# Summing the modulation vectors over the partitions by accumulating DMAs instead of by products with ones, in the first FFN of a two-layer diffusion backbone

## The chip, the cores and the metric

The kernel runs on one core of a Trainium2 chip. The metric is the device time of one execution in microseconds (us). The kernel before takes 1251.65 us, the median of three runs (1251.4 to 1252.48).

The engines are named as in the profile: PE is TensorE (PEld its weight loads), DVE is VectorE, ACT is ScalarE, POOL is GpSimd, and SP is the engine from whose queue nearly all DMAs are issued. SBUF is the on-chip memory with 128 partitions; PSUM holds the matmul results.

## The reference, cut to what matters

Two layers work on 256 latent tokens and, in the first layer, on 256 context tokens, all with 1024 channels, in float32. Each layer is a half-step SwiGLU FFN, a mixer (neighbourhood attention in layer 0, a short gated convolution in layer 1), and a second half-step FFN. Every sub-layer is modulated by vectors made from a conditioning vector:

```python
s_c, s_cc = silu(c), silu(c_ctx)
for i in range(2):
    m  = (s_c  @ ada_w[i] + ada_b[i]).reshape(1, 9, 1, 1024)    # for latent tokens
    mc = (s_cc @ ada_w[i] + ada_b[i]).reshape(9, 1024)          # for context tokens (layer 0)
    # sub-layer j uses shift m[3j], scale m[3j+1], gate m[3j+2]
    x = layer_norm(alpha * x + w * gate * f(x * (1 + scale) + shift))
```

So a modulation vector is a sum over 1024 input channels: one row of 1024 numbers for each of the nine parts of a layer, and in layer 0 parts 0 to 4 are needed for both conditionings. `ada_w` is 1024 x 9216 floats a layer, 37.7 MB. The FFN of layer 0 maps 1024 channels to 2 x 2816 and back.

## The kernel before, in words

**Precision.** A float32 matrix product is made of three faster matmuls. Each weight tile is split into a high part (ACT writes `w1h`, `w2h`, L216) and a remainder (DVE writes `w1l`, `w2l`, L219), and PE runs high x high, low x high and high x low. So every weight that PE uses has passed ACT and DVE first, in halves of 128x512.

**The first FFN.** It runs over 512 tokens (latent and context together). Its 22 column blocks of 128 are cut into panels (p0 has three blocks, the others two or one). For each block PE fills two banks `f` (L720), 48 matmuls of 512 columns; then ACT and DVE make the gated product: `sil` (L730) and its split `gh`, `gl` (L118, L119). The panels form three parts: p0 to p3 (eight blocks), p4 to p7 (eight) and p8 to p10 (six). After each part comes the product with the second weight matrix into eight banks `w` (L170 to L173), each of which DVE adds to the residual stream, multiplied by the gate vector (`res`, `x`, `xc`, L411 and L416).

**The background stream.** While this runs, the remaining modulation vectors are made in the background by `ada`, seven groups of two vectors, in this order: (part 2 of layer 0, both conditionings), (part 3, both), (part 4, both), (parts 5 and 6), (parts 7 and 8), (parts 0 and 1 of layer 1), (parts 2 and 3 of layer 1). For each vector eight tiles `ar` of 128 x 1024 are loaded (512 KB each, L312), and DVE multiplies each by a column of the silu'd conditioning and adds it to an accumulator `acc` of 128 x 1024 (L301 for the first, L303 for the others). In groups 1 to 3 one load serves both vectors. What is left is a sum over the 128 partitions of `acc`: matmuls with a 128x32 tile of ones on PE (L338), four for a group, DVE adds the bias (L339), and two DMAs write the two rows to a scratch in DRAM, `scr` (L341). Readers of `scr` are the gate loads (`gate`, L784 and L370) and the loads of columns (`mrow`, L385). In the later sub-layers the same sums are made by `sum_up`, with a partition reduction on POOL (L349) and a DMA that adds one row to `scr` (L350), where the bias was put before (L1153).

**What sets the order.** PE's order is the order in which the code is written: the stream is a generator that is stepped by `tick`, once for every six matmuls, at a rate of 0.44 to 0.6 steps a tick, and each `yield` in `ada` is one step. On DVE, ACT, POOL and SP a scheduler orders the instructions ahead of time; each engine then runs its list in order, and an instruction that waits holds up those behind it. `acc` tiles come from a ring of two buffers, `ar` tiles from three; a tile is written again only when its last reader is done. The raw weight tiles have four buffers.

## Time and profile before

| What | Value |
|---|---|
| Median of three runs | 1251.65 us |
| The profiled execution | 1251.97 us, of which the span from first to last instruction is 1250.2 us |
| PE busy | 1229.4 us (98%) |
| DVE busy | 965.3 us (77%) |
| ACT busy | 645.2 us (52%) |
| POOL busy | 82.4 us (7%) |
| Bytes moved by DMA | 275.67 MB, mean 221 GB/s |
| Stretch of the first FFN's stream | about 54 to 365 us |

The tables of the profile give busy time, count and mean length of one; a timeline row gives start and length in us, and merges neighbours of one kind (its last field is the count). Lengths in a timeline overlap a little where the next one starts before the last has drained, so the distance between starts is what an engine can do. An idle time in square brackets is that just before the row, with what ended it. Names are those of the program without buffer numbers; L303 is line 303.

### The profile page before, as it was taken

The page shows a single profiled execution, that of the slowest core. Times are in us where ns is not written, and L with a number is a line of the kernel's source. Part 1 is how long each engine was busy: PE and PEld are TensorE (multiplying, and loading weights), DVE is VectorE, ACT ScalarE, POOL GpSimd, SP SyncE. Part 2 cuts the span into 40 slices and gives each one's busy share as a digit, 9 for nine tenths or more (in the row PEclk, how much of TensorE's full clock was granted, in tenths as well). Part 3 has the DMA queues.
Part 4 walks back from the last instruction along what each step waited for, and adds up shares of the span by engine and source line. Part 5 has one row for each costly group of instructions (what it writes and reads, how often), then busy time and mean ns, then how long its engine had stood idle before and what let it go on. Part 6 is the DMA issues. An engine that isn't in the chain of part 4 may idle for free.

```text
span 1250.2 us, 17238 instructions
## 1 busy us (share of the span) xinstructions
PE 1229.4 (98%) x5794; PEld 994.1 (80%) x5794; DVE 965.3 (77%) x1675; ACT 645.2 (52%) x1233; POOL 82.4 (7%) x85
## 2 busy tenths in 40 slices
PE   8999999999999999999999999999999999999997
PEld 5787778778778878777888878888878887888886
DVE  3598987888878867888877866877777798878646
ACT  2433132322325556587678535678635644677631
POOL 0000000000001011120000200020010020002000
PEclk9999999999999999999999999999999999999999
DMA  9877679778852654554899876899886775899941
GB/s 295 301 241 235 183 236 303 248 263 277 278 186 80 183 119 85 113 110 144 262 295 290 256 252 197 218 283 300 274 266 186 222 225 159 220 294 245 276 153 68
DMA packets 232304, 275.67 MB, mean 221 GB/s; under 512 B 59622, under 2 KB 178910, under 8 KB 232216
## 3 DMA queue, kind: packets, MB, share of 16 engines
q1 hardware_dynamic: 232020, 274.54, 73.3%
q8 instruction: 45, 0.74, 0.2%
q14 instruction: 43, 0.35, 0.1%
q0 software_dynamic: 160, 0.02, 0.1%
q10 hardware_dynamic: 36, 0.02, 0.0%
HBM read 265.27 MB, written 2.20 MB: 214 GB/s over the span
## 4 chain that ended last, share of the span: by engine, by line
PE 83%; DVE 6%; DMA 4%; ACT 3%; issue 2%; SPq 1%; POOL 0%; DVEq 0%; ACTq 0%
PE f L720 19%; PE w L171 17%; PE w L170 17%; PE w L173 16%; DMA ar<-in_ada_w_dram 3%; PE wc L170 2%; PE wc L171 2%; PE wc L173 2%; PE wkv L170 1%; PE wkv L171 1%; PE wkv L173 1%; PE hT L446 1%; DVE w2l L219 1%; ACT pr L1023 1%; PE S L1015 1%
## 5 line engine op out<-in xcount | busy, mean ns | idle before, releaser
L219 DVE TENSOR_TENSOR w1l<-w1r,w1h 128x512 fp32r<-128x512 f32 (+1 forms) x352 | 230.0, 697 | 47.7 <-ACT w1h L216 46.5
L216 ACT ACTIVATE w1h<-w1r 128x512 fp32r<-128x512 f32 (+1 forms) x352 | 198.7, 618 | 115.6 <-DMA w1r<-in_ffn_w_in_dram 64.4
L170 PE MATMUL w<-w1h,hTh 128*128 128x512 f32 x528 | 206.3, 391 | 1.2 <-ACT hTh L118 1.2
L171 PE MATMUL w<-w1l,hTh 128*128 128x512 f32 x528 | 205.7, 390 | 0.0
L303 DVE SCALAR_TENSOR_TENSOR acc<-ar,cst,acc 128x512 f32<-128x512 f32 x266 | 186.9, 745 | 15.1 <-DMA ar<-in_ada_w_dram 15.0
L171 PE MATMUL w<-w2l,gh 128*128 128x512 f32 (+1 forms) x446 | 172.8, 388 | 3.6 <-DVE w2l L219 3.6
L216 ACT ACTIVATE w2h<-w2r 128x512 fp32r<-128x512 f32 x176 | 101.6, 624 | 143.3 <-PE w L173 107.8
L170 PE MATMUL w<-w2h,gh 128*128 128x512 f32 (+1 forms) x446 | 173.5, 390 | 0.0
L219 DVE TENSOR_TENSOR w2l<-w2r,w2h 128x512 fp32r<-128x512 f32 x176 | 118.2, 710 | 59.1 <-ACT w2h L216 58.3
L173 PE MATMUL w<-w1h,hTl 128*128 128x512 f32 x528 | 162.6, 389 | 0.0
L173 PE MATMUL w<-w2h,gl 128*128 128x512 f32 (+1 forms) x446 | 136.2, 386 | 0.0
L720 PE MATMUL f<-h0h,w1h 128*128 128x512 f32 x352 | 132.8, 393 | 1.0 <-ACT w1h L216 0.6
L720 PE MATMUL f<-h0l,w1h 128*128 128x512 f32 x352 | 133.2, 391 | 0.0
L720 PE MATMUL f<-h0h,w1l 128*128 128x512 f32 x352 | 132.8, 390 | 0.0
L170 PEld LDWEIGHTS w<-w1h,hTh 128*128 128x128 f32 x528 | 99.1, 188 | 22.4 <-ACT hTh L118 2.1
L173 PEld LDWEIGHTS w<-w1h,hTl 128*128 128x128 f32 x528 | 99.1, 188 | 20.9
L171 PEld LDWEIGHTS w<-w1l,hTh 128*128 128x128 f32 x528 | 99.1, 188 | 20.6 <-DVE w1l L219 0.3
L171 PEld LDWEIGHTS w<-w2l,gh 128*128 128x128 f32 x446 | 83.8, 188 | 22.3 <-DVE w2l L219 6.0
L170 PEld LDWEIGHTS w<-w2h,gh 128*128 128x128 f32 x446 | 83.8, 188 | 19.2 <-issue 1.7
L173 PEld LDWEIGHTS w<-w2h,gl 128*128 128x128 f32 x446 | 83.3, 188 | 17.0
L720 PEld LDWEIGHTS f<-h0h,w1h 128*128 128x128 f32 x352 | 65.5, 188 | 19.5 <-issue 4.2
L720 PEld LDWEIGHTS f<-h0l,w1h 128*128 128x128 f32 x352 | 65.6, 188 | 14.3 <-issue 1.0
(193 smaller groups left out, 1765.0 us busy)
## 6 DMA issues: line engine op xcount, KB each, us to landing
w1r<-in_ffn_w_in_dram SPq DMA_DIRECT2D x340, 256.0 KB
ar<-in_ada_w_dram SPq DMA_DIRECT2D x128, 512.0 KB
w2r<-in_ffn_w_out_dram SPq DMA_DIRECT2D x88, 512.0 KB
ar<-in_ada_w_dram SPq DMA_DIRECT2D x32, 256.0 KB
wkvr<-in_na_w_qkv_dram SPq DMA_DIRECT2D x32, 256.0 KB
wcr<-in_sc_w_in_dram SPq DMA_DIRECT2D x32, 256.0 KB
wqr<-in_na_w_qkv_dram SPq DMA_DIRECT2D x8, 512.0 KB
wor<-in_na_w_out_dram SPq DMA_DIRECT2D x8, 512.0 KB
```

Of the source, the lines that this page charges most:

```text
L170: nc.tensor.matmul(ps, lh, rh, start=first and i == 0, stop=False)
L171: nc.tensor.matmul(ps, lh, rl, start=False, stop=False)
L173: nc.tensor.matmul(ps, ll, rh, start=False, stop=last and i == n - 1)
L216: last_split[:] = [nc.scalar.activation(hi[:, a:a + m // W_HI], raw[:, a:a + m // W_HI], AF.Copy)]
L219: nc.vector.tensor_tensor(out=lo[:, a:b], in0=raw[:, a:b], in1=hi[:, a:b].bitcast(F32), op=ALU.subtract)
L303: nc.vector.scalar_tensor_tensor(out=a, in0=src, scalar=sc, in1=a, op0=ALU.mult, op1=ALU.add)
L446: nc.tensor.transpose(ps[:, k * P:(k + 1) * P], z[h][:, k * P:(k + 1) * P], ident)
L720: nc.tensor.matmul(ps, w, hT0[k][part == 1], start=(k == part == 0), stop=(k == KC - 1 and part == 1))
L1015: nc.tensor.matmul(banks[i], (qh, qh, ql)[f][ps, qs], (kh, kl, kh)[f][ps, :], start=f == 0, stop=f == 2)
L1023: nc.scalar.activation(pr, S, AF.Exp, bias=mx[:, 0:1], accum_out=mx[:, 1:2])
```

## The change

In the first FFN the sum over the partitions no longer goes through PE. When the last of the eight products of a vector is in `acc`, POOL issues a tree of DMAs that add one half of the partitions of `acc` to the other half, in place: 64 rows onto 64, then 32, 16, 8, 4, 2 and 1, each waiting for the one before it; and one more that adds the remaining row to `scr`. The two vectors of groups 1 to 3 are issued alternately. The bias is put into `scr` at the start by three DMAs from DRAM to DRAM. The tile of ones, the bias tiles, the result rows, and the DVE additions and DMAs that served them are gone, and so are three of the four steps after each group. The ring of `acc` has three buffers now.

```diff
-                        acc[i] = hp.tile([P, D], F32, tag="acc", bufs=2, name=nm("acc"))
+                        acc[i] = hp.tile([P, D], F32, tag="acc", bufs=2 if on_pool[0] else 3, name=nm("acc"))
...
-            if on_pool[0] and k == KC - 1:
-                sums.extend((vec, acc[i]) for i, vec in enumerate(vecs) if vec[:2] == (l, m))
+            if k == KC - 1:
+                ready = [(vec, acc[i]) for i, vec in enumerate(vecs) if vec[:2] == (l, m)]
+                if on_pool[0]:
+                    sums.extend(ready)
+                    return
+                n = P // 2
+                while n:
+                    for _, a in ready:
+                        nc.gpsimd.dma_start(a[0:n], a[n:2 * n], accum_op=ALU.add)
+                    n //= 2
+                for (l, m, v), a in ready:
+                    nc.gpsimd.dma_start(scr[l][v:v + 1, m * D:(m + 1) * D], a[0:1], accum_op=ALU.add)
...
-        n = 2 * len(vecs)
-        if not bias_rows:
-            bias_rows.append(hp.tile([P, 512], F32, tag="adab", name=nm("adab")))
-            nc.gpsimd.memset(bias_rows[0], 0.0)
-        bt = bias_rows[0]
-        for i, (l, m, v) in enumerate(vecs):
-            sync.dma_start(bt[64 * i:64 * i + 64:32], ada_b[l, m * D:(m + 1) * D].rearrange("(a b) -> a b", b=512))
         yield 1
-        yield 1
-        yield 1
-        rows = hp.tile([P, 512], F32, tag="adar", name=nm("adar"))
-        ps = tpb("ada")
-        for i in range(len(vecs)):
-            for h in range(2):
-                j = 2 * i + h
-                nc.tensor.matmul(ps[32 * j:32 * j + 32, :], ones, acc[i][:, h * 512:(h + 1) * 512], start=True, stop=True)
-        nc.vector.tensor_tensor(out=rows[:32 * n], in0=ps[:32 * n], in1=bt[:32 * n], op=ALU.add)
-        for i, (l, m, v) in enumerate(vecs):
-            sync.dma_start(scr[l][v, m * D:(m + 1) * D].rearrange("(a b) -> a b", b=512),
-                           rows[64 * i:64 * i + 64:32, :])
-        yield 1
...
-    ab0 = hp.tile([P, D], F32, tag="acc", bufs=2, name="ab0")
+    ab0 = hp.tile([P, D], F32, tag="acc", bufs=2 if on_pool[0] else 3, name="ab0")
...
+    for l, v, r in ((0, 0, slice(2 * D, 9 * D)), (0, 1, slice(2 * D, 5 * D)), (1, 0, slice(0, 9 * D))):
+        sync.dma_start(scr[l][v, r].rearrange("(a b) -> a b", a=16), ada_b[l, r].rearrange("(a b) -> a b", a=16))
...
-    sync.dma_start(scr[1][0, 4 * D:9 * D].rearrange("(a b) -> a b", a=16), ada_b[1, 4 * D:9 * D].rearrange("(a b) -> a b", a=16))
```

PE's list loses the 28 products with ones and is otherwise the same. The lists of DVE, POOL and SP are rearranged around them. Numbers in the names below count tiles; line numbers of the change are those of its own file, where L300 is the multiply-and-add into `acc`, L298 its first product, L219 still the remainder of the weights, L717 `sil`, L398 `res` and L403 the addition to `x`.

DVE in the change, near the end of p3 and the first product with the second matrix. `acc_158` is the second accumulator of group 2; it takes the buffer that held the first accumulator of group 1, `sil0_182` and `gl_184` belong to the last block of p3, and `w2_190` is the first bank of the product.

```order
L717 TENSOR_TENSOR sil0_182_1155<-sil0_182_1155,f0_180_1108 128x512 [waits PE_49]
L219 TENSOR_TENSOR w2l_222_1371<-w2r_220_1369,w2h_221_1370 128x512 [waits DMAHW7_49,Activation_49]
L298 TENSOR_SCALAR acc_158_956<-ar_156_951,cst_88 128x512 [waits DMASW4_49,DMASW6_49,DMASW2_49,DMASW0_49]
L298 TENSOR_SCALAR acc_158_956<-ar_156_951,cst_88 128x512
L300 SCALAR_TENSOR_TENSOR acc_158_956<-ar_163_979,cst_88,acc_158_956 128x512 [waits DVE_49] x2
L300 SCALAR_TENSOR_TENSOR acc_158_956<-ar_164_997,cst_88,acc_158_956 128x512 [waits DVE_49] x2
L119 TENSOR_TENSOR gl_184_1159<-sil0_182_1155,gh_183_1158 128x512 [waits Activation_49]
L219 TENSOR_TENSOR w2l_222_1371<-w2r_220_1369,w2h_221_1370 128x512
L398 SCALAR_TENSOR_TENSOR res_203_1231<-w2_190_1174,gate_185_1162 128x512 [waits DMAHW4_49,PE_49]
```

The first products of `acc_158` wait for POOL's DMAs (DMASW), and `gl_184` now stands behind them; before, both accumulators of group 2 began together, some eighteen rows ahead of the same `sil`.

DVE in the change, at the last bank of that product (`w2_240`, whose `res` is `res_242`). `acc_199` is the second accumulator of group 3; its buffer held the first accumulator of group 2. `w1l_279` and `w1l_282` belong to p5.

```order
L219 TENSOR_TENSOR w1l_279_1754<-w1r_277_1752,w1h_278_1753 128x512 [waits DMAHW5_49,DMAHW4_49,Activation_49]
L298 TENSOR_SCALAR acc_199_1214<-ar_197_1209,cst_88 128x512 [waits DMASW4_49,DMASW6_49,DMASW2_49,DMASW0_49]
L298 TENSOR_SCALAR acc_199_1214<-ar_197_1209,cst_88 128x512
L300 SCALAR_TENSOR_TENSOR acc_199_1214<-ar_205_1241,cst_88,acc_199_1214 128x512 [waits DVE_49] x2
L300 SCALAR_TENSOR_TENSOR acc_199_1214<-ar_206_1259,cst_88,acc_199_1214 128x512 [waits DVE_49] x2
L398 SCALAR_TENSOR_TENSOR res_242_1538<-w2_240_1509,gate_186_1164 128x512 [waits PE_49]
L219 TENSOR_TENSOR w1l_282_1763<-w1r_280_1761,w1h_281_1762 128x512 [waits DMAHW7_49,DMAHW6_49,Activation_49]
L300 SCALAR_TENSOR_TENSOR acc_198_1211<-ar_209_1287,cst_88,acc_198_1211 128x512 [waits DMAHW4_49]
```

Group 3's second accumulator begins only here, just ahead of the last `res` of the product; before, both accumulators of group 3 began together and five of their eight pairs of products stood ahead of that `res`. Behind these rows follow the remaining products of group 3 and all but one of the eight products of the first vector of group 4 (`acc_233`), and then, still on DVE:

```order
L300 SCALAR_TENSOR_TENSOR acc_233_1457<-ar_257_1588,cst_88,acc_233_1457 128x512 [waits DVE_49]
L219 TENSOR_TENSOR w1l_285_1772<-w1r_283_1770,w1h_284_1771 128x512
L300 SCALAR_TENSOR_TENSOR acc_233_1457<-ar_258_1604,cst_88,acc_233_1457 128x512 [waits DMAHW1_49,DVE_49]
L300 SCALAR_TENSOR_TENSOR acc_233_1457<-ar_258_1604,cst_88,acc_233_1457 128x512 [waits DVE_49]
L219 TENSOR_TENSOR w1l_288_1781<-w1r_286_1779,w1h_287_1780 128x512
L219 TENSOR_TENSOR w1l_282_1763<-w1r_280_1761,w1h_281_1762 128x512
L219 TENSOR_TENSOR w1l_279_1754<-w1r_277_1752,w1h_278_1753 128x512
L717 TENSOR_TENSOR sil0_274_1745<-sil0_274_1745,f0_270_1700 128x512 [waits PE_49]
```

The second half of `w1l_279`, which the second pair of matmuls of p5 reads, has moved behind 34 multiply-and-adds that follow `res_242`; before, both halves of p5's first two tiles stood ahead of group 4's first product, and the rest behind five of its multiply-and-adds.

5 lines of the change are left out of this document (1 added, 4 removed).

## The prediction, made before the change was timed

> **What bounds the kernel now.** I read the busy times first, then the chain that ended last, then the stretches of the first FFN.
>
> ```profile
> PE 1229.4 (98%) x5794; PEld 994.1 (80%) x5794; DVE 965.3 (77%) x1675; ACT 645.2 (52%) x1233; POOL 82.4 (7%) x85
> PE 83%; DVE 6%; DMA 4%; ACT 3%; issue 2%; SPq 1%; POOL 0%; DVEq 0%; ACTq 0%
> ```
>
> PE sets the end. The table by stretches (span, then busy time and count of PE, PEld, DVE, ACT, POOL, then clock, DMA share, GB/s) shows how near DVE is to it where the change lies:
>
> ```profile
> 100.00:135.00 35.00, 35.00 (x156) 28.98 (x155) 33.00 (x53) 9.95 (x18) 0.00 (x0) 1.00 0.74 238
> 135.00:175.00 40.00, 40.00 (x183) 31.27 (x182) 38.45 (x62) 9.83 (x18) 0.00 (x0) 1.00 0.68 202
> 175.00:220.00 45.00, 45.00 (x201) 37.22 (x200) 35.86 (x57) 13.92 (x24) 0.00 (x0) 1.00 0.86 284
> ```
>
> PE never stops there, at full clock. DVE is busy 94% and 96% in the first two: whatever it is made late by, it can't catch up. POOL does nothing.
>
> The third view is DVE's own order of time, at the three places that decide.
>
> ```profile
> 87.39 2.73 DVE L303 SCALAR_TENSOR_TENSOR acc<-ar,cst,acc 128x512 f32<-128x512 f32 x4
> 98.76 0.49 DVE L301 TENSOR_SCALAR acc<-ar,cst 128x512 f32<-128x512 f32 x1 [2.95 <-PE ada L338]
> 100.94 4.72 DVE L303 SCALAR_TENSOR_TENSOR acc<-ar,cst,acc 128x512 f32<-128x512 f32 x7
> 119.49 0.69 DVE L119 TENSOR_TENSOR gl<-sil,gh 128x512 fp32r<-128x512 f32 x1
> 161.77 0.68 DVE L411 SCALAR_TENSOR_TENSOR res<-w,gate 128x512 f32<-128x512 f32 x1
> 169.59 2.49 DVE L219 TENSOR_TENSOR w1l<-w1r,w1h 128x512 fp32r<-128x512 f32 x4
> 181.37 2.49 DVE L219 TENSOR_TENSOR w1l<-w1r,w1h 128x512 fp32r<-128x512 f32 x4
> ```
>
> Group 1's sums are complete at about 90.1 (the first vector's at 88.7). A buffer of `acc` that isn't free stops DVE (98.76: it waited for the products with ones). One multiply-and-add takes 4.72/7, about 0.66 us of the queue; a weight remainder, from the four in 2.49, 0.60; a first product 0.40. The last four remainders of p5 (its third and fourth tile) ended at 183.8; PE, which began p4 at 161.19 (row below), came to them after 96 matmuls, one group's products with ones and 12 more matmuls, at about 187: three us of slack are all that DVE had there.
>
> **What the change removes.** PE's rows at group 1:
>
> ```profile
> 97.09 0.39 PE L720 MATMUL f<-h0h,w1l 128*128 128x512 f32 x1
> 97.31 0.39 PE L720 MATMUL f<-h0l,w1h 128*128 128x512 f32 x1
> 97.63 1.06 PE L338 MATMUL ada<-acc,ones 128*32 128x512 f32 x8
> 98.63 0.50 PE L720 MATMUL f<-h0h,w1h 128*128 128x512 f32 x1
> 98.96 0.39 PE L720 MATMUL f<-h0h,w1l 128*128 128x512 f32 x1
> L338 PE MATMUL ada<-acc,ones x56: 592/605/617, 97.6 to 362.5; 128*32 128x512 f32 x56
> ```
>
> Matmuls start 0.227 us apart (97.09 to 97.31). From 97.31 to 98.96 pass 1.65 us, where two distances, 0.45, would have passed: one group costs PE 1.20 us, though its eight passes last 0.6 us each, since they overlap. Seven groups: **8.4 us** off the path that sets the end, because PE is never idle there. That is the whole gain. DVE loses seven bias additions of 0.6 us, too.
>
> **What the change adds: the tree.** The nearest row is the DMA that adds one row to the scratch in the later sub-layers (POOL's time for it, and from issue to landing):
>
> ```profile
> L350 POOL DMA_DIRECT2D scr<-red x5: 997/997/1118, 713.1 to 1147.6; - x5
> DMA to landing us min/median/max: 3.3/3.8/4.2
> ```
>
> A vector needs seven such steps in SBUF and one to `scr`, each waiting for the landing before. From below: POOL issues 16 DMAs for the pair, 16 x 0.997 = 16 us, if landing were hidden behind the other vector's issue. From above: 8 x 4.2 = 33.6, and the large steps move two times 127 rows of 4 KB, 1.04 MB, which is 3.7 us at 284 GB/s and twice that if destinations are read as well as written: 41 us. I take 8 x 3.3 = 26.4, the quick end since seven of eight write to SBUF, and half of 3.7 for the vector's own share: **28 us** from the last product to a free buffer. The tree's data itself, 14 x 0.52 = 7.3 MB, is small beside the 275.67 MB moved.
>
> The Trainium skill ("DMA: Bandwidth & Descriptors", section "Anatomy of one DMA — SWDGE (gpsimd) path") puts a DMA of this kind at about 2.0 us plus its bytes at 436 GB/s. By that the tree would last an estimated 8 x 2.0 + 1.2 = 17 us; what 17 us would make of the kernel is the first rival below. The row above, 3.3 us at the least for 4 KB, speaks for the longer one.
>
> Who waits for a tree: the ring has three buffers, and one of them held the bias at the start, so group 2's second accumulator needs group 1's first, and group 3's second needs group 2's first. DVE's list holds remainders and gated products behind each (the order above).
>
> *Place 1, group 2.* The tree of group 1 ends at 88.7 + 28 = 116.7. DVE gets to the waiting row at about 116.4 anyway, behind `sil`. Then 2 x 0.40 + 4 x 0.66 + 0.6 to `gl`: 120.8. PE needs it for the last matmul of the first bank of `w`, before the change 116.45 + 23 x 0.227, now 1.2 earlier: 120.5.
>
> ```profile
> 116.45 0.39 PE L170 MATMUL w<-w2h,gh 128*128 128x512 f32 x1
> 161.19 0.39 PE L720 MATMUL f<-h0h,w1h 128*128 128x512 f32 x1
> ```
>
> So 0.3 us of stall; each us of a longer tree costs one here.
>
> *Place 2, group 3.* The remaining five loads of group 2 wait in SP's queue behind the gate loads, which wait for the same tree; gate and `ar` loads of 0.5 MB at 284 GB/s take 1.9 us each, so group 2's first vector is complete some 19.5 us later, at 136.2, its tree at 164.2. There DVE waits with the last `res` and p5's remainders behind it: 0.8 + 2.6 for the buffer's first products, then from `res` to the second half of `w1l_279` 34 multiply-and-adds, two first products and 11 others, 22.5 + 0.8 + 6.6 = 29.9. It is done at 197.5. PE wants it at: 115.25 (first matmul of `w`) + 43.5 (192 matmuls) + 21.8 (96 of p4) + 0.9 = 181.4. Stall **16 us**, place 1 included. Without any wait for a tree `res` would start at 159.1, when PE ends its last bank, and the remainder be done at 189: 7.6 us would stay, since group 3 has slid behind the product.
>
> *Place 3, group 4.* Group 3's first vector is complete 16.6 us after 164.2, its tree at 209; the second accumulator of group 4 waits for it, and so do SP's column loads with five `ar` loads behind them. About 15.5 us on, at 224.5, the last remainder of p6 is done, which PE wants at 181.4 + 24.8 = 206.2: **18 us** in all, 2 more than at place 2.
>
> *Behind that* the ring is long enough: a vector of groups 4 to 7 lasts eight loads, 15 us, and its buffer is wanted two vectors later, 30 us. But three steps less after each group push the stream together: 88 loads in 95 steps instead of 116 (one step a load, and one instead of four after each of seven groups), beside DMA that is already 86% busy. From nothing, as 95 steps still fit, to 8 us, about four loads' time that DVE would wait; I take **4**.
>
> ```profile
> L312 SPq DMA_DIRECT2D ar<-in_ada_w_dram x88: 323/331/651, 44.9 to 347.6; - x88
> ```
>
> *Hidden:* the three bias DMAs stand among the first loads of the FFN, 84 KB in all; POOL's issues have an idle engine; its later work (`rs`) starts after the last tree.
>
> **The sum.** 1251.97 - 8.4 + 18 + 4 = 1265.6; against the median, which lies 0.3 below the profiled execution, about **1265**. With trees of 23 to 33 us the places give 11 to 33 us, and with 0 to 8 behind them the time is 1255 to 1285.
>
> **The rivals.**
>
> *A short tree, 17 us.* POOL's 16 issues bound it, landing hidden. Then nothing waits at place 1; group 2 is complete at 135.9, its tree at 153, before DVE gets there; the 7.6 us of place 2 remain by the order alone, and 0 to 4 behind: 1251.97 - 8.4 + 7.6 + 2 = **1253**. For it: POOL's 0.997 us. Against it: no landing under 3.3. It is also what the Trainium skill's fit, named above, would give.
>
> *All of it hidden, faster.* DVE takes the rows of place 2 in time: that needs group 3's loads some 8 us sooner than I lay them, or PE's demand for p5 later. Then only the gain is left: 1251.97 - 8.4 = **1243.6**. For it: DVE is 80% busy from 175 to 220, and PE waited for nothing before. Against it: the three us of slack that p5 had, and 24 more multiply-and-adds ahead of p5's remainders. It decides if PE's idle time in the first FFN stays under 8 us.
>
> *A long tree, 40 us.* If the 64- and 32-row steps share the 16 DMA engines with the weights at half speed: place 1 at 128.7 stalls 12, place 2 at 188.2 stalls 40, place 3 at 245 some 54: 1251.97 - 8.4 + 54 + 4 = **1302**. For it: the DMA share of 0.74 to 0.86. Against it: 3.8 us in the median at such shares.
>
> **How the numbers follow.** My forecast has 60%, the short tree 17%, the hidden one 13%, the long one 10%. Under 0.2% of the time, 2.5 us, a change can't be told from none. The forecast's and the long tree's 70% are slower, of the short tree's 17% I count 8 as slower, 7 as the same and 2 as faster; the hidden case is faster: 0.15 faster, 0.07 the same, 0.78 slower. The range holds the forecast (1255 to 1285), the short tree and part of the long one: 1249 to 1290; the hidden case and the longest trees are left out.
>
> **What would show it.** The groups of waits should name DVE's first products (`acc`) as waiting for DMAs of `acc` or `scr`, some 8 us at the start of group 3 and some at group 4; PE idle for `w1l` at p5, 181 to 198, about 16 us, and little at p6. POOL should show 112 DMAs in pairs about 3.5 us apart; 28 us from a group's last product to the landing in `scr` is the number everything hangs on. I am wrong if PE shows no idle time between 150 and 230, if DVE reaches p5's remainders before 182, or if trees end within 20 us and the kernel is still much slower: then it is the denser stream or POOL's issues on DVE's ports.

## The result, and the profile after

The kernel with the trees takes **1319.1 us** (median of six runs, 1314.8 to 1323.6), the kernel before beside it 1251.9 (1251.4 to 1254.2): the ratio is 1.0535, with a 95% interval of 1.0511 to 1.0559. It is slower, as predicted, but by 67 us where 13 were forecast; 1319 lies outside the range (1249 to 1290).

The profiled execution took 1323.62 us, its span 1321.8 us. The busy times, the row of PE's granted clock, the software DMA queue and the chain that ended last, from the page of the kernel after:

```profile
PE 1242.9 (94%) x5738; PEld 1006.0 (76%) x5738; DVE 963.1 (73%) x1667; ACT 646.1 (49%) x1233; POOL 171.2 (13%) x196
PEclk9998897898999999999999999999999999999998
q0 software_dynamic: 4640, 7.37, 3.7%
PE 62%; DMA 17%; DVE 11%; issue 4%; ACT 3%; POOL 1%; SPq 1%; DVEq 0%; ACTq 0%; POOLq 0%
```

The chain was 83% PE and 4% DMA; now 17% of it is DMA. PE's clock, which was full all through, has dents in slices 4 to 10, which is the first FFN.

Where in the program the time went is read from three landmarks: the start of the last matmul of the first FFN's panels (tile `f`), the start of the last matmul of all (tile `w`), and the end of the span. Every run below is in the table; times in us, of the one execution that was profiled (of the change the slowest of its six, of e16 the slowest of its ten).

| Run | last `f` | from there to the last `w` | from there to the end |
|---|---|---|---|
| before | 361.7 | 880.1 | 8.4 |
| **after** | **426.3** | **881.9** | **13.6** |
| e1: four accumulators | 397.3 | 878.4 | 13.6 |
| e2: before, 36 activation tiles | 359.9 | 881.5 | 7.8 |
| e3: before, dense stream | 378.4 | 879.0 | 7.8 |
| e4: pause at p5 filled | 422.5 | 880.5 | 13.6 |
| e5: four steps | 410.1 | 885.9 | 13.6 |
| e6: four accumulators and steps | 400.9 | 880.2 | 13.6 |
| e7: one level | 387.6 | 879.6 | 8.0 |
| e8: trees for groups 2, 4, 6, 7 | 379.7 | 879.6 | 10.2 |
| e9: before, idle trees | 374.9 | 888.4 | 13.6 |
| e10: its control | 362.0 | 884.3 | 7.9 |
| e11: narrow trees | 425.9 | 879.0 | 13.5 |
| e12: narrow, four accumulators and steps | 385.7 | 888.0 | 13.5 |
| e13: before, narrow idle trees | 363.1 | 886.9 | 13.5 |
| e14: before, four pauses | 391.9 | 881.6 | 7.8 |
| e15: trees for groups 2 and 7 | 377.2 | 879.3 | 8.0 |
| e16: before, three accumulators | 367.1 | 881.1 | 8.0 |
| e17: e6, slower pace | 394.8 | 881.3 | 13.6 |
| e18: e15, slower pace | 362.1 | 895.5 | 8.0 |

Of the 71.6 us between the two spans, 64.6 arise in the first FFN, 1.8 behind it, and 5.2 at the very end.

What PE waited for in the first FFN, from the groups of waits between 50 and 460 us of the kernel after (total, times, longest); the kernel before has no wait of PE in this stretch. Behind them the eight longest pauses themselves, from PE's order of time:

```profile
PE f L707 <- DVE w1l L219: 26.8, 4, 16.6
PE w L170 <- ACT w2h L216: 8.1, 2, 4.5
PE w L173 <- DVE gl L119: 7.8, 1, 7.8
PE f L707 <- ACT w1h L216: 5.3, 2, 4.2
PE w L171 <- DVE w2l L219: 4.3, 2, 4.1
```

```profile
129.36 0.79 PE L173 MATMUL w<-w2h,gl 128*128 128x512 f32 x1 [7.81 <-DVE gl L119]
154.64 0.80 PE L171 MATMUL w<-w2l,gh 128*128 128x512 f32 x1 [4.13 <-DVE w2l L219]
215.35 0.79 PE L707 MATMUL f<-h0h,w1l 128*128 128x512 f32 x1 [16.59 <-DVE w1l L219]
249.88 0.79 PE L707 MATMUL f<-h0h,w1l 128*128 128x512 f32 x1 [7.09 <-DVE w1l L219]
279.12 0.79 PE L707 MATMUL f<-h0h,w1h 128*128 128x512 f32 x1 [4.25 <-ACT w1h L216]
306.07 0.54 PE L170 MATMUL w<-w2h,gh 128*128 128x512 f32 x1 [4.54 <-ACT w2h L216]
312.84 0.80 PE L170 MATMUL w<-w2h,gh 128*128 128x512 f32 x1 [3.54 <-ACT w2h L216]
360.44 0.50 PE L707 MATMUL f<-h0h,w1l 128*128 128x512 f32 x1 [2.93 <-DVE w1l L219]
```

The five groups add up to 52.3 us. The first row of the pauses is place 1 of the prediction, the third is place 2 (p5), the fourth place 3 (p6); the other five are at places that it had not named. Most first matmuls last about 0.8 us instead of 0.39. The stretches behind two of the pauses show why (length, PE's busy time and count, granted clock, DMA share, which adds up the packets' times and can pass 1, and GB/s):

```profile
215.30:218.00 2.70, 2.65 (x6) 0.50 0.87 295
218.00:222.00 4.00, 4.00 (x13) 0.62 1.04 290
222.00:226.00 4.00, 4.00 (x19) 1.00 1.08 286
249.80:254.00 4.20, 4.12 (x10) 0.50 0.88 275
```

After a pause PE's granted clock is half for three to six us. The clock's shortfall times the length, over the stretches behind all eight pauses, is 16 us. Six of the seven groups of products with ones stood ahead of the last `f`, and PE is 1 us late already at 50 us. So the account of the first FFN is 52.3 idle + 16 at low clock - 7.2 for the products removed + 1 = 62, of 64.6; some 2 us are not accounted for.

The trees on POOL, in its order of time (start and POOL's own time, then idle time ahead), and DVE's first products for the second accumulators of groups 2, 3 and 4, with the rows around that of group 3:

```profile
90.70 2.74 POOL L310 DMA_DIRECT2D acc<-acc  x2 [89.08 <-DVE acc L300]
124.60 0.77 POOL L313 DMA_DIRECT2D scr<-acc  x1 [0.82 <-DMA acc<-acc]
144.37 0.82 POOL L310 DMA_DIRECT2D acc<-acc  x1 [19.00 <-DVE acc L300]
172.11 1.64 POOL L313 DMA_DIRECT2D scr<-acc  x2 [0.71 <-DMA acc<-acc]
194.30 0.82 POOL L310 DMA_DIRECT2D acc<-acc  x1 [20.56 <-DVE acc L300]
```

```profile
125.17 0.88 DVE L298 TENSOR_SCALAR acc<-ar,cst 128x512 f32<-128x512 f32 x2 [7.39 <-DMA scr<-acc]
172.76 3.36 DVE L219 TENSOR_TENSOR w1l<-w1r,w1h 128x512 fp32r<-128x512 f32 x5 [0.66 <-ACT w1h L216]
176.05 0.88 DVE L298 TENSOR_SCALAR acc<-ar,cst 128x512 f32<-128x512 f32 x2
179.49 0.68 DVE L398 SCALAR_TENSOR_TENSOR res<-w,gate 128x512 f32<-128x512 f32 x1
235.29 0.88 DVE L298 TENSOR_SCALAR acc<-ar,cst 128x512 f32<-128x512 f32 x2 [4.69 <-DMA acc<-acc]
```

By the landings in the trace, group 1's tree lasts from 90.7 to 125.0 (34 us), group 2's first vector's from 144.4 to its landing in `scr` at 174.3 (30), group 3's first vector's from 194.3 to 235.2 (41). I had said 28.

DVE stood for a tree at places 1 and 3, 7.4 and 4.7 us. At place 2 it did not: it came to the row at 176.05 straight from the remainders, 1.7 us after that tree had landed. So the longest pause, 16.6 us at p5, is not a wait for a tree. It is the sum of three things. PE ended the product's last bank at about 176.1, and `res` starts 3.4 us later, behind the first products of `acc_199`. From `res` to the end of the remainder, at 215.3, DVE waits 5.3 us in all for `ar` loads. The other 30.5 us are work that stands between the two, 7.8 more than the 22.7 us after which PE asked for the remainder (at 198.8). 3.4 + 5.3 + 7.8 = 16.5.

### The profile page after: what moved, and what is told of

It reads as the page before. It is cut to its first block, busy times and chain, and to the rows that moved or that the text cites. A ratio compares the mean times of both kernels' runs of the same rounds, so it can differ in the third digit from the quotient of the medians.

```text
span 1321.8 us, 17256 instructions
## 1 busy us (share of the span) xinstructions
PE 1242.9 (94%) x5738; PEld 1006.0 (76%) x5738; DVE 963.1 (73%) x1667; ACT 646.1 (49%) x1233; POOL 171.2 (13%) x196
## 3 DMA queue, kind: packets, MB, share of 16 engines
q0 software_dynamic: 4640, 7.37, 3.7%
## 4 chain that ended last, share of the span: by engine, by line
PE 62%; DMA 17%; DVE 11%; issue 4%; ACT 3%; POOL 1%; SPq 1%; DVEq 0%; ACTq 0%; POOLq 0%
PE w L171 14%; PE w L170 14%; PE w L173 14%; DMA acc<-acc 11%; PE f L707 6%; DVE acc L300 3%; DMA ar<-in_ada_w_dram 3%; PE wkv L170 2%; PE wkv L171 2%; PE wkv L173 2%; DMA w1r<-in_ffn_w_in_dram 2%; PE wc L170 1%; PE wc L171 1%; PE wc L173 1%; DVE w1l L219 1%
## 5 line engine op out<-in xcount | busy, mean ns | idle before, releaser
L219 DVE TENSOR_TENSOR w1l<-w1r,w1h 128x512 fp32r<-128x512 f32 (+1 forms) x352 | 231.1, 700 | 59.3 <-ACT w1h L216 58.5
L300 DVE SCALAR_TENSOR_TENSOR acc<-ar,cst,acc 128x512 f32<-128x512 f32 x266 | 185.3, 746 | 33.7 <-DMA ar<-in_ada_w_dram 33.6
L171 PE MATMUL w<-w2l,gh 128*128 128x512 f32 (+1 forms) x446 | 176.7, 397 | 9.0 <-DVE w2l L219 9.0
L170 PE MATMUL w<-w2h,gh 128*128 128x512 f32 (+1 forms) x446 | 176.3, 396 | 8.1 <-ACT w2h L216 8.1
L219 DVE TENSOR_TENSOR w2l<-w2r,w2h 128x512 fp32r<-128x512 f32 x176 | 118.4, 711 | 74.1 <-ACT w2h L216 73.1
L707 PE MATMUL f<-h0h,w1l 128*128 128x512 f32 x352 | 136.8, 402 | 26.8 <-DVE w1l L219 26.8
L173 PE MATMUL w<-w2h,gl 128*128 128x512 f32 (+1 forms) x446 | 139.6, 394 | 7.8 <-DVE gl L119 7.8
L707 PE MATMUL f<-h0h,w1h 128*128 128x512 f32 x352 | 136.3, 403 | 5.7 <-ACT w1h L216 5.3
L707 PE MATMUL f<-h0l,w1h 128*128 128x512 f32 x352 | 136.1, 400 | 0.0
L310 POOL DMA_DIRECT2D acc<-acc x98 | 80.2, 862 | 308.3 <-DMA acc<-acc 178.5
L171 PEld LDWEIGHTS w<-w2l,gh 128*128 128x128 f32 x446 | 85.7, 192 | 30.4 <-DVE w2l L219 13.5
L707 PEld LDWEIGHTS f<-h0h,w1l 128*128 128x128 f32 x352 | 68.0, 194 | 43.0 <-DVE w1l L219 28.9
```

Source lines behind the costliest of these rows:

```text
L170: nc.tensor.matmul(ps, lh, rh, start=first and i == 0, stop=False)
L171: nc.tensor.matmul(ps, lh, rl, start=False, stop=False)
L173: nc.tensor.matmul(ps, ll, rh, start=False, stop=last and i == n - 1)
L219: nc.vector.tensor_tensor(out=lo[:, a:b], in0=raw[:, a:b], in1=hi[:, a:b].bitcast(F32), op=ALU.subtract)
L300: nc.vector.scalar_tensor_tensor(out=a, in0=src, scalar=sc, in1=a, op0=ALU.mult, op1=ALU.add)
L310: nc.gpsimd.dma_start(a[0:n], a[n:2 * n], accum_op=ALU.add)
```

## The experiments

Edits are to the kernel after, where nothing else is said. The theory to test was the prediction's: **(A)** DVE's list stands in front of a buffer that a tree still holds, and PE waits behind DVE. Its rivals: **(B)** the denser stream, **(C)** the clock as a cost of its own, and **(F)** the trees' bytes on the DMA engines.

### Four accumulators, and the room for them (e1, e2)

```diff
-NACT = 38
+NACT = 36
-... tag="acc", bufs=2 if on_pool[0] else 3, ...
+... tag="acc", bufs=2 if on_pool[0] else 4, ...
```

> The change with a ring of four accumulators instead of three; the room is taken from the ring of activation tiles (36 instead of 38, in the whole kernel). Theory A, the ring: PE's pauses of the first FFN come from DVE's row of work standing in front of a buffer that a tree still holds (16.6 us at p5, 7.1 at p6, 7.8 at the first product). A fourth buffer gives every tree one more vector's time, so the pauses before 250 us go, and with them some 40 to 50 us of the 67 lost: 1255 to 1275 us. What would stay comes from the later groups, whose trees follow one another on POOL's queue (249 to 417 us for eight vectors, 21 us each, against some 15 us of loads). Rival B, the denser stream and the trees' own traffic: the buffers don't matter, the time stays above 1300 us, and DVE waits for ar loads (28.8 us before 460 us) as long as it did.

> Control for the run with four accumulators: the kernel before with 36 instead of 38 activation tiles, nothing else. If those two tiles are not short anywhere the time is that of before, 1251.9 us within 3; whatever it differs by is taken off the other run before that is read. All theories expect no difference.

With four, 1290.4 us (ratio 1.0299, 1.0281 to 1.0317); the control 1251.7 (0.9997, 0.9988 to 1.0007), so the tiles are free. The fourth buffer takes 29 us off, all in the first FFN (426.3 to 397.3). That is as (A) has it, but it is less than the 40 to 50 expected, and DVE's list is another one too. DVE's groups of waits with four accumulators say what came in place of the buffers:

```profile
DVE acc L300 <- DMA ar<-in_ada_w_dram: 32.6, 24, 3.2
DVE acc L298 <- DMA ar<-in_ada_w_dram: 6.9, 4, 4.4
DVE acc L298 <- DMA scr<-acc: 5.3, 1, 5.3
```

Waits for a tree fell from 19.7 us (in the kernel after 7.4, 4.7, 5.8 and 1.7, at 125, 235, 294 and 339 us) to 5.3, and those for `ar` loads rose from 30.6 to 39.5; before the change they were 14.7.

### The dense stream, and the old spacing (e3, e5, e6)

e3 is the kernel before with three `yield 1` fewer after a group; e5 the change with four instead of one; e6 that with four accumulators.

> The kernel before, with products with ones as they were, but one step of the background stream after each group instead of four, as the change has it. Theory B, the stream: loads and multiply-adds pushed together delay the weights and their remainders, and this alone makes a good part of the 67 us: 1270 to 1300 us. Theory A, the ring: without a tree no buffer is held long; I laid 0 to 8 us at this and took 4: 1252 to 1260 us, PE without pauses of more than 2 us before 250 us.

> The change, with four steps of the background stream after each group, as the kernel before has them; three accumulators as in the change. With four accumulators the pairs' trees ran one behind the other on POOL (issues from 88.8, 126.4, 163.9 us on, some 37 us a pair), and groups of 16 loads come in a little less than that. Theory A, now with the tree's rate: the trees are the slow belt, and whatever gives a group more time helps: with steps back to before's, groups come some 38 us apart and a tree just fits, but with three accumulators the second vector of each group still asks for a buffer whose tree began only when the group ahead was complete: 1270 to 1295 us. Rival B, the stream's density: undone, the time falls to 1250 us or less.

> Both: four accumulators (36 activation tiles, which cost nothing by themselves) and four steps after each group. Theory A: every tree has a group's time and more before its buffer is wanted again, no pause of PE over 2 us before 250 us, 1243 to 1258 us; 1243.6 would be the full gain of the seven products. Rival F, the trees' traffic: 98 transfers within SBUF take the DMA engines (share 0.95 from 200 to 350 us with four accumulators, 0.82 before) and delay loads whatever the ring: above 1270 us, with DVE waiting for ar loads 25 us or more.

e3: 1267.3 (1.0121, 1.0105 to 1.0136), between what the two theories expected. But its PE waits for no weights at all. It waits for the products with ones, which now come too soon behind the last multiply-and-add; the only wait in the profile's group table that counts is this:

```profile
PE ada L335 <- DVE acc L303: 5.9, 3, 3.7
```

The change has no such products, so e3 says nothing against the dense stream there. e5: 1312.6 (1.0471, 1.0446 to 1.0495), e6: 1297.0 (1.0348, 1.0331 to 1.0365). Spacing the groups takes 6 us off with three accumulators and adds 7 with four: neither expectation for e5 held (1270 to 1295, and 1250 or less), and that of (A) for e6, 1243 to 1258, fell flat. DVE waits 58 us for `ar` loads in e6, as (F) said, and 7.3 us for a gate load that stands behind the first tree in SP's queue. Its DMA engines from 100 to 350 us, by queue (packets, MB, share of the 16 engines):

```profile
q1 hardware_dynamic: 28343, 59.40, 74.7%
q0 software_dynamic: 3264, 5.23, 13.0%
```

The trees take 13.0% for 5.23 MB, the loads 74.7% for 59.4 MB: per byte a tree's packets take twice as long.

### The tree's length and its bytes (e7, e11, e12)

```diff
 # e7: after the first level
-                    n //= 2
+                    break
...
 # e11, and e12 with four accumulators and four steps
-                        nc.gpsimd.dma_start(a[0:n], a[n:2 * n], accum_op=ALU.add)
+                        nc.gpsimd.dma_start(a[0:n, 0:64], a[n:2 * n, 0:64], accum_op=ALU.add)
```

> The change with only the first of the seven levels of each tree, the one of 64 rows, and the addition to the scratch; the sum over the other 63 rows is left out, so this is no longer the same sum. Ring of three and the dense stream as in the change. A tree lasts about 6.5 + 3 = 10 us then instead of 35 to 40, though it still moves half of the tree's bytes. Theory A: the tree's duration is the cause; the time is 1244 to 1256 us, no wait of DVE for a buffer. Rival B, the stream's density: 1265 us or more, as the stream is as dense as in the change. Rival F, the trees' bytes: of the 67 us about half stays, 1285 us.

> The change, with each DMA of a tree's levels cut to 64 of 1024 columns; the other columns are not summed, the addition to the scratch is whole. The number of steps, the waits, the ring of three and the dense stream are those of the change, but the trees' bytes are about a sixteenth. Theory F, traffic: most of the 67 us goes, 1245 to 1260 us. Theory A, the chain of landings: a step's landing is 2.0 us at the least, so a pair's tree still lasts 8 x 2.0 to 8 x 3.3 = 16 to 26 us, place 2 (group 3's second accumulator) still stalls: 1253 to 1275 us, and PE's longest pause is for a remainder at p5. If bytes and not steps had made the trees long, POOL's issues show a pair's tree in 20 us or less.

> Four accumulators, four steps after each group and trees of 64 of 1024 columns (the other columns are not summed). The same with whole trees took 1297 us, and the order of DVE and ACT is the same but for a few rows. Theory G, two causes that hide each other (the buffers' waits and the trees' bytes): with both cured 1243 to 1256 us, DVE waits for ar loads 15 us or so as before, not 58. Rival: bytes are not it, and what is left in the run with whole trees comes from SP's and POOL's queues (gate loads that wait for a tree, 8.9 and 6.4 us, 112 issues): 1275 us or more.

e7: 1276.6 (1.0193, 1.0178 to 1.0208). Six of a tree's eight steps gone, 42 us back, more than by any other single cut, and still 24 above before. (A)'s 1244 to 1256 missed; the time lies between (B)'s bound of 1265 and (F)'s 1285.

e11: **1318.0** (1.0522, 1.0500 to 1.0544): a sixteenth of the bytes, and nothing gained, where (F) expected 1245 to 1260 and (A) 1253 to 1275. Its trees are shorter. Group 1's lasts 27 us, in the order of time of POOL, then of DVE, then PE's first pause, of e11:

```profile
88.50 1.15 POOL L310 DMA_DIRECT2D acc<-acc  x1 [86.89 <-DVE acc L300]
114.45 0.77 POOL L313 DMA_DIRECT2D scr<-acc  x1 [0.22 <-issue]
```

```profile
115.62 0.89 DVE L298 TENSOR_SCALAR acc<-ar,cst 128x512 f32<-128x512 f32 x2 [7.94 <-DMA scr<-acc]
121.54 13.34 DVE L300 SCALAR_TENSOR_TENSOR acc<-ar,cst,acc 128x512 f32<-128x512 f32 x20 [1.79 <-DMA ar<-in_ada_w_dram]
134.79 0.68 DVE L717 TENSOR_TENSOR sil<-sil,f 128x512 f32<-128x512 f32 x1
```

```profile
136.19 0.79 PE L170 MATMUL w<-w2h,gh 128*128 128x512 f32 x1 [16.19 <-ACT gh L118]
```

DVE gets its buffer at 115.6, ten us sooner than in the change. But the scheduler, which made the list anew for the other DMAs, has put 20 multiply-and-adds between it and `sil`, and PE's first pause is 16.2 us instead of 7.8. All pauses together are 54.2 us, against 52.3. So a shorter tree isn't a shorter stall: what stands behind the waiting row is decided ahead of time. DVE's groups of waits in e11 show both causes at work:

```profile
DVE acc L298 <- DMA scr<-acc: 53.1, 8, 9.5
DVE acc L300 <- DMA ar<-in_ada_w_dram: 11.0, 12, 2.0
```

With the bytes gone, DVE's waits for `ar` loads fell from 30.6 us to 11.6, and those for a tree rose from 19.7 to 53.1: as far as these waits tell, with three accumulators the buffers take what the bytes give back.

e12 has all but the order of e6 and 1289.8 us (1.0293, 1.0279 to 1.0306), where the theory of two causes hiding each other expected 1243 to 1256. In the first FFN the bytes give back 15.2 us (400.9 to 385.7); behind it 7.8 are lost again, where rows of POOL that the next normalization needs stand behind a tree (DVE's `x` waited 8.9 us for `rs`). In the first FFN 24 us over before remain. Two pauses make 15.3 of them: 8.2 us at place 1, where DVE waited 9.4 us for group 1's tree, since the stream comes sooner with four buffers, and 7.1 at 343 us.

### Trees that nobody waits for (e9, e10, e13)

The kernel before without the extra weight pair (`ext = [0, 0]`, e10), and with seven pairs of trees on two tiles of their own, whole (e9) and narrow (e13):

```diff
...
+        for a in junk:
+            nc.gpsimd.tensor_tensor(out=a[0:1, 0:1], in0=rows[0:1, 0:1], in1=rows[0:1, 0:1], op=ALU.subtract)
+        n = P // 2
+        while n:
+            for a in junk:
+                nc.gpsimd.dma_start(a[0:n], a[n:2 * n], accum_op=ALU.add)
+            n //= 2
...
```

> The kernel before, sums by products with ones as they were, and beside them seven pairs of trees that nobody waits for: the same 112 DMAs of POOL, same sizes, on two tiles of their own, each pair started when a group's sum is read off; their results are not used. Room for the two tiles comes from the extra pair of weight tiles of the first FFN; the control below has that alone. Theory F, traffic: the trees take the 16 DMA engines 13.0% of the time from 100 to 350 us (with four accumulators and four steps), on top of the weights' 75 to 79%, so that loads come late and DVE, in order, with them; with nobody waiting for a tree the time still grows by 20 us or more over the control. Theory A, buffers and waits alone: within 4 us of the control.

> Control: the kernel before without the extra pair of weight tiles in the first FFN. Both theories: somewhat slower than before if at all, 1252 to 1265 us; only its difference from the run with idle trees counts.

> The kernel before without the extra weight pair, beside it the idle trees with 64 of 1024 columns (their results are not used in any case). The control took 1256.5 us, whole idle trees 1279.9. Theory F, bytes: 1256 to 1260 us. Rival: the number of POOL's DMAs and their issuing: 1270 us or more.

Control 1256.5 (1.0036, 1.0024 to 1.0048), whole idle trees 1279.9 (1.0214, 1.0194 to 1.0235), narrow ones 1265.7 (1.0090, 1.0069 to 1.0110). So 23 us with nobody waiting, and the table splits them: 12.9 in the first FFN, of which narrow trees leave 1.1; 4.1 and 2.6 behind it; and 5.7 and 5.6 at the end, bytes or no bytes. (That end is why e13 lies above the 1256 to 1260 of (F).) **(F) is shown**, with 12 us of bytes in the first FFN (15 in e6 against e12). DVE's wait for the multiply-and-adds' loads is in the groups of waits, first of e10, then of e9:

```profile
DVE acc L303 <- DMA ar<-in_ada_w_dram: 16.0, 18, 1.9
```

```profile
DVE acc L305 <- DMA ar<-in_ada_w_dram: 30.3, 22, 4.0
```

### What a pause costs (e4, e14)

e4 fills the change's pause at p5 with 15 matmuls; e14 puts four pauses into the kernel before:

```diff
+    def pause():                                  # e14, ahead of p2, p4, p6 and p8
...
+        nc.tensor.matmul(dm, w, m, start=True, stop=True)
...
+        nc.scalar.activation(pz, dm, AF.Copy)
+        for _ in range(5):
+            nc.scalar.activation(pz, pz.bitcast(F32), AF.Copy)
...
+        nc.tensor.matmul(dm, w, pz, start=True, stop=True)
```

> The change, with 15 more matmuls of 128x512 in full f32 into an unused PSUM bank put in PE's list of p5, where it paused 16.6 us (198.4 to 215.4); their results are not used. They are to fill most of the pause, so that PE comes out of it at full clock: after the pause the matmuls lasted 0.63 to 0.79 instead of 0.39 us, and the granted clock was 0.50 from 215.3 to 218 and 0.62 to 222, which is 0.5 x 2.7 + 0.38 x 4 = 2.9 us of lost time. Theory C, the lost clock counts in full: p6's pause stays 7.1 us, everything behind p5 comes 2.9 us sooner, 1316 us instead of 1319. Rival D, it is absorbed: what PE waits for at p6 comes when it comes (249.9 us), the pause there grows by about 3 us and the end stays, 1319 us. That difference is less than the runs of the change scatter (1314.8 to 1323.6), so the places are read in the trace: where p6 starts, and how long PE waited there.

> The kernel before (36 activation tiles, which cost nothing) with four pauses of PE: at the start of p2, p4, p6 and p8 one more matmul, six copies of its 128x512 result on ACT, one behind the other, and a second matmul that needs the last. The results are not used. Each pause should last some 3.5 to 5 us. Theory C, the clock: each pause costs itself and some 2 to 3 us of matmuls at half the granted clock, so four pauses of 4 us cost 24 to 28 us: the time grows by about 1.6 times the idle time that the trace shows. Rival D: it grows by the idle time alone, about 16 us.

e4 was inconclusive: 1318.8 us, and the fill fell short, so that PE paused 5.4 us more and came out of it at a clock of 0.50 as well. e14 settles it: 1282.9 (1.0240, 1.0224 to 1.0255), 29.6 us more than before. In PE's order of time these are the only pauses:

```profile
87.70 0.80 PE L773 MATMUL dm<-pz,h0h 128*128 128x512 f32 x1 [5.53 <-ACT pz L771]
173.69 0.66 PE L773 MATMUL dm<-pz,h0h 128*128 128x512 f32 x1 [4.66 <-ACT pz L771]
226.01 0.80 PE L773 MATMUL dm<-pz,h0h 128*128 128x512 f32 x1 [5.24 <-ACT pz L771]
323.65 0.50 PE L773 MATMUL dm<-pz,h0h 128*128 128x512 f32 x1 [4.66 <-ACT pz L771]
```

They add up to 20.1 us and cost 29.6, nearer to the 1.6 times that (C) expected than to the 20 of its rival. The granted clock accounts for 8.5 us of the difference, half of the time that it was at 0.50 behind the four; the rest is about what the eight added matmuls take. So each pause of about 5 us costs some 2 us on top, 1.4 times its length in all.

### Few trees (e8, e15)

Products with ones for the other groups, four accumulators, four steps:

```diff
+TREES = ((0, 3), (0, 5), (0, 6), (1, 0), (1, 1), (1, 2), (1, 3))   # e8; e15: ((0, 3), (1, 2), (1, 3))
+                if (l, m) not in TREES:
+                    return
...
```

> Trees for groups 2, 4, 6 and 7 alone; groups 1, 3 and 5 summed by products with ones as before (their sums added to the scratch by POOL's DMA, since the bias lies there already), four accumulators, 36 activation tiles, four steps after each group. Each tree has then two groups' time. The gain is at most 4 x 1.2 = 4.8 us. Theory A: 1246 to 1252 us, perhaps better than both kernels. Rival F, traffic: half of what four accumulators with all trees lose.

> Trees for groups 2 and 7 alone, where the DMA engines have room (share 0.69 to 0.78 from 100 to 200 us, 0.35 after 350 us), products with ones for the rest, four accumulators, four steps. The most that it can gain is 2 x 1.2 = 2.4 us. Theory G: nothing waits, 1249.5 to 1252 us, faster or the same. If even that is slower than 1254, trees cost something that neither buffers nor bytes explain.

e8: 1269.2 (1.0122, 1.0093 to 1.0150); e15: **1269.2** (1.0115, 1.0095 to 1.0135). Two trees cost as much as four. Neither the buffers (DVE waits for none in e15) nor the bytes explain that. The expectation of (A) for e8 and that for e15 failed; half of what e6 lost, as (F) had it for e8, would be 22 us, and e8 lost 17. In e15's trace PE's longest pause, 4.6 us at 335.1, is for `w1l`, which stands on DVE behind products of group 7 that waited 8.6 us for `ar` loads. DVE waited 37.3 us for `ar` loads in all, against 14.7 before the change.

### The throttle (e16, e17, e18)

In SP's list of e15 more `ar` loads stand ahead of the weights than before the change, though the steps are the same. Two accumulators and the product that frees them may have held the stream back. e16 gives the kernel before a third accumulator (36 activation tiles); e17 and e18 slow the stream of e6 and e15:

```diff
-            background[1] = 0.44
+            background[1] = 0.36
-ADA_SLOW, ADA_FAST, ADA_SLOWEST = 3, 0.6, 0.115
+ADA_SLOW, ADA_FAST, ADA_SLOWEST = 3, 0.4, 0.115
```

> The kernel before with a third accumulator, as the change has it (36 activation tiles for the room, which cost nothing by themselves), and nothing else: products with ones, no trees. In SP's queue 65, 83 and 103 loads of summands then stand ahead of the 64th, 80th and 96th weight load, against 59, 78 and 97. Theory T, the throttle: two accumulators held the stream back; a third lets loads crowd in ahead of the weights, DVE waits some 25 to 30 us for ar loads instead of 15 and stands ahead of remainders with them: 1258 to 1270 us. Rival: a buffer more can only help or do nothing, 1250 to 1254 us; then it is POOL's few DMAs that cost 17 us in the run with two trees.

> Whole trees, four accumulators, four steps, and a slower pace of the stream (0.36 and 0.40 steps instead of 0.44 and 0.6), so that 59, 85 and 102 loads stand ahead of the 64th, 80th and 96th weight load instead of 65, 86 and 104. Without the pace it took 1297 us. Theory T: the pace takes off 10 to 20 us, 1275 to 1287 us; the trees' bytes, 23 us in the run with idle trees, stay. Rival: no difference, 1295 us.

> Trees for groups 2 and 7 alone, four accumulators, four steps, and the slower pace (59, 85 and 98 loads ahead of the 64th, 80th and 96th weight load). Without the pace it took 1269 us. Theory T: 1250 to 1258 us. Rival, POOL's DMAs as such: 1265 us or more.

e16: 1254.7 (1.0012, 1.0002 to 1.0022). A third buffer alone costs a little, not the 6 to 18 us expected, though DVE's waits for `ar` loads rose to the 26 us that the throttle had foretold. e17: 1290.8 (1.0294, 1.0275 to 1.0314), 6 us less than e6 where 10 to 20 were expected. e18: 1267.1 (1.0112, 1.0090 to 1.0135); by its time the pace did nothing, as the rival said (1265 or more), but the landmarks tell another story. The first FFN's panels end at 362.1 us, as before the change (361.7), 15 us sooner than in e15: up to there the pace took the whole loss away, although DVE waited 36.6 us for `ar` loads, hardly less than in e15. The time was lost again right behind it (895.5 against 879.3): some 3.6 us at a pause of 2.4 us for `gh` at 368 us, and some 9 us from 390 to 415 us, at the start of the next sub-layer. POOL's and DVE's order of time in e18:

```profile
395.62 0.80 POOL L315 DMA_DIRECT2D acc<-acc  x1 [2.37 <-DMA acc<-acc]
396.16 0.47 POOL L433 TENSOR_TENSOR rs<-mv,lnc 128x1 f32<-128x1 f32 x1
```

```profile
390.28 0.21 DVE L431 BATCH_NORM_AGGREGATE mv<-st 128x2 f32<-128x12 f32 x1
397.32 1.01 DVE L444 TENSOR_SCALAR x<-x,mv,rs 128x512 f32<-128x512 f32 x2 [6.83 <-POOL rs L434]
```

`mv` is there at 390.5, but `rs`, the normalization's factor, stands on POOL behind a step of group 7's tree that waits for a landing, and starts at 396.2; PE paused 4.4 us for `x` and came out of it at half clock. The slower pace had pushed that tree past the FFN's end. So in e18 POOL's DMAs do cost time, by their place in POOL's queue.

No version with trees beats the kernel before.

## Why the prediction was right or wrong

**Right: the mechanism at places 1 and 3.** A buffer held by a tree stops DVE, and PE waits for what stands behind: for `gl` at the first product, where DVE stood 7.4 us and PE paused 7.8, and for `w1l` at p6, where DVE stood 4.7 and PE paused 7.1. That such waits are a cause, e1 and e11 show: 29 us less with a fourth buffer, and 53.1 us of DVE's waits for trees where the bytes are gone.

**Wrong: the wait at place 2; the 16 us there came out by luck.** At p5 PE paused 16.6 us; the prediction's 16, less the 0.3 of place 1, gave 15.7. But it had DVE stand 5 us for group 2's tree, from 159.1 (PE's last bank) to 164.2, and then 29.9 us of work. In the trace DVE waited for no tree there; it waited 5.3 us for `ar` loads instead, a term that the sum did not have at this place. The two errors cancel, and what was right is the order: DVE's list, in which group 3 has slid behind the product. The sign "some 8 us at the start of group 3" did not come.

**Wrong: the tree's duration, 28 us.** It was 34, 30 and 41 in the first three groups. At place 1, where I had said that each further us costs one, the tree ended 8.3 us later than predicted and cost 7.5: 7.8 instead of 0.3. By the fit of the Trainium skill ("DMA: Bandwidth & Descriptors", section "Anatomy of one DMA — SWDGE (gpsimd) path") the estimate was 17. Even e11's narrow trees, 64 columns wide, took 27 for eight steps, 3.4 a step: the trace does not agree with that estimate, and the row that I set against it, 3.3 at the least, was the better one.

**Wrong: "each us of a longer tree costs one here" as a rule.** e11 had the very tree that I had predicted, 27 us, and 54.2 us of pauses. I had read the stalls from one list of DVE; another tree makes another list. The prices held for that list alone.

**Wrong: "behind that the ring is long enough", 4 us.** Pauses after p6 (4.25, 4.54, 3.54, 2.93 and smaller ones) come to 17 us, with place 3 at 7.1 instead of 2 and a pause of 4.1 at 154.6 for `w2l` that I had not seen. DVE also stood for trees there, 5.8 and 1.7 us. And a term left out is the trees' bytes: I had called them "small beside the 275.67 MB moved", but their packets take twice the time per byte, and in a stretch (100 to 350 us) where the loads' packets alone hold 75% of the engines (e6) to 79 (before). e9 prices it at 12 us in the first FFN where nobody waits, e12 at 15. (Of no weight: the three bias DMAs move 76 KB, not 84.)

**Left out: the clock.** The sum counted each pause at its own length. The granted clock fell behind every long one; 16 us in the change, and e14 shows it by itself. The Trainium skill has it ("TensorE: Matmul & The Clock Gate", section "What's actually happening"): PE's clock is gated to half after an idle window of about 3.4 us and comes back after a busy one. The trace agrees for the long pauses: behind them the clock stays at 0.50 for 2.9 to 5.8 us from PE's restart and is full after that.

**Left out: the program's end.** 5.2 us more pass behind the last matmul, of which the prediction had no word (below).

**The account of the miss**, in the profiled executions, 1323.6 against 1265.6, 58 us: pauses 30.3 (52.3 instead of 0.3 + 15.7 + 2 + 4 = 22), low clock 16, the end 5.2, behind the FFN 3 (1.8 after the 1.2 that the seventh group's products give back there), the start 1, and some 2 not accounted for.

**The rivals.** The long tree (1302) was nearest in time, but by the wrong prices: it had 54 us of stalls from trees of 40, at three places; the chip had 52 from trees of 30 to 41, at nine. It had 10%, and the range ended at 1290. The short tree (1253) had no case on the chip: e7, with a tree of one level, still took 1277. Its bound was too high, too: POOL took 0.80 us for one of these DMAs in the median, not 0.997. "All hidden" fell with the first pause.

**What stays open.** The causes are not a sum. Removing buffers' waits gives 29 us, removing bytes gives nothing with three accumulators and 15 in the FFN with four, the pace 6 or 15. Each cure moved the wait to the next thing: `ar` loads, SP's queue, `rs` on POOL. Each run also had a DVE list of its own, and none kept the list of the change and altered the waits alone, so that what the order costs by itself is read from the trace at p5 (8 us) and not from an experiment. That the crowding of loads ahead of weights is the rest of it is argued from e18's landmark, where the pace removed it, and not shown: a third buffer alone does not make it (e16), and DVE's waits for `ar` loads were as long in e18 as in e15. What else sets e15 apart from e16, two trees, a fourth buffer, sums added by POOL's DMA and a bias laid down early, was not separated.

## What to carry to other kernels

Work moved off the bounding engine has to be followed to what it holds: a buffer, a place in a queue, bytes; the gain here was 8.4 us, and the bytes alone cost 12. Price a pause of PE of some five us at 1.4 times its length. When a stall comes out as long as predicted, look whether the wait that was predicted is there: at p5 it was not. And don't carry a stall's price from one built order to another, since a scheduler makes the list anew. When a change shows as one number, cut the span at landmarks first: a run that looked like "no effect" (e18) had cured the stage in question and lost the same time in the next one.

## What was not expected of the hardware

**The clock after short pauses.** PE's granted clock can also fall after pauses much shorter than those of e14. In e16 the only pause over 1 us in the first FFN, 1.41 us at 258.4, was followed by a clock of 0.51 from 259.8 to 263.2; pauses of 1.22 us at 209.0 in e15 and of 1.49 at 208.8 in e18 were not. In e15, after one of 1.97 us that followed one of 1.18 five us earlier, PE's first matmul lasted 0.80 us, and the clock from 260 to 275 us was 0.77 (the stretch's row has its length, DVE's busy time, clock, DMA share, GB/s):

```profile
261.38 0.80 PE L171 MATMUL w<-w2h,gh 128*128 128x512 f32 x1 [1.97 <-ACT gh L119]
```

```profile
260.00:275.00 15.00, 12.15 (x21) 0.77 0.88 280
```

**Accumulating DMAs within SBUF take twice the packet time of a load per byte**: 13.0% for 5.23 MB against 74.7% for 59.40 MB in e6. Packets of one size, 4096 bytes, took 327 ns in the median on the trees' queue and 159 ns on that of the loads, in the same stretch. Their landings in the change, from the list of POOL's issues at L310:

```profile
DMA to landing us min/median/max: 2.0/4.4/8.5
```

The prediction had taken 3.3 from additions to the scratch.

**The end of the program grows with the number of POOL's DMAs.** From the last matmul to the end of the span pass 7.8 to 8.4 us in programs with 5 to 47 DMAs issued by POOL, 10.2 in e8 with 75, and 13.5 or 13.6 in every program with 117, whatever their bytes (0.54 MB in e11, 7.37 in the change). What grows is a DRAIN at the end of POOL's list, an instruction of its sequencer, which the busy times leave out. The rows of the closing line, first of the change, then of before (minimum, median, maximum in ns):

```profile
L1264 POOLq DRAIN  x3: 40/102/10555, 1310.5 to 1321.6; - x3
L1276 POOLq DRAIN  x3: 40/93/1408, 1244.0 to 1249.9; - x3
```

The longest of the three took 1.41 us with 5 DMAs, 3.69 with 33 (e7), 4.85 with 47 (e15), 7.13 with 75 and 10.55 with 117: from 33 on, 0.08 us for each DMA. Up to 47 it ends about when the output's DMAs are done, and costs next to nothing.
